# Delta net preparation: sums of squares from transposed tiles, by ScalarE squares, GpSimd halving additions and a VectorE reduction

## Chip, cores, metric

One core of a Trainium2 chip. The metric is the device time of one execution in microseconds (us), the median of several runs.

## What is computed

One inference step of a hybrid decoder layer for 1024 prompt tokens and 8 decode tokens. The change lies in the gated delta net, in the preparation of its 4 heads of width 128 (the sequence in 8 chunks of 128 tokens here):

```
def l2norm(a):
    return af * lax.rsqrt(jnp.sum(af * af, axis=-1, keepdims=True) + NORM_EPS)
q = l2norm(qkv[..., :GDN_WIDTH].reshape(bsz, T, GDN_HEADS, GDN_HEAD_DIM))
k = l2norm(qkv[..., GDN_WIDTH:2 * GDN_WIDTH].reshape(bsz, T, GDN_HEADS, GDN_HEAD_DIM))
...
L = jnp.where(strict, jnp.einsum('nbhid,nbhjd->nbhij', k_beta, k) * decay, 0.0)
sol = lax.linalg.triangular_solve(L + jnp.eye(C, dtype=f32), rhs, left_side=True, lower=True,
                                  unit_diagonal=True)
qk = jnp.where(tri, jnp.einsum('nbhid,nbhjd->nbhij', q, k) * decay, 0.0)
```

The kernel does not normalise `q` and `k` themselves. It needs, for each token and head, the sum of squares of the query and of the key (`ssq`, `ssk`, one column of 128 tokens per chunk), and puts the factors in later.

## The kernel before

The layer runs in stages: input projections and convolutions together with the S5 part (to about 239 us), the preparation of the delta net (239 to 277), the inversion of the triangular blocks with the `z` projection beside it (to about 328), the merge of the inverted blocks, the chain over the chunks, output projection, norm and the two feed-forward products (to 1273).

`mixers` (line 1210) sets the order around the change. It weaves `gdn_prep` for the 4 heads with the rest of the last convolution tile, `conv_tile(11)` (line 1217): each `yield` of `gdn_prep` gives a cost, and for 0.3 of it the convolution may put in matmuls, in groups of three (lines 155 to 157). Then come `gdn_invert` (line 396), the `z` tiles woven with `gdn_values` (line 1221), and `gdn_merge` (line 436). PE runs in the order written out (a manual schedule, line 1308); the other engines' queues are ordered by the framework's scheduler. SP's queue, which issues the DMAs, is in order too.

`gdn_prep` works on each head in two halves of 4 chunks, so on 8 halves in turn. A half does this:

1. PE transposes 4 chunks of the queries into a PSUM bank `pc`; ScalarE squares each of the four 128x128 blocks and accumulates along the row into `ssq` (line 337). The squares themselves go into a scratch tile `pt` that nobody reads; it is one buffer for both engines that use it.
2. PE transposes the broadcast decay column into a second bank `pc`; ScalarE takes four Relu (line 347), GpSimd subtracts the mask (line 349), ScalarE takes the exponential (line 350): the tile `d2`.
3. PE computes keys by keys and keys by queries, 2 chunks to a bank (lines 359, 360). VectorE multiplies the keys-by-keys block with the identity and accumulates along the row, which gives the diagonal, `ssk` (line 363, four instructions a half).
4. VectorE works out the small factors of 4 columns (lines 368 to 372), GpSimd the power `n4` (line 373), and VectorE scales and masks the products into the tile `uq` (line 377, four instructions a half).

There are 2 banks for `pc`, 4 for the products (`psum(2, 4, 2)`, line 1306), 4 buffers of `d2`. A bank of products is free when `uq` has been written from it.

In `gdn_invert` SP stores the diagonal blocks of `uq` to memory (`du`, 4 DMAs a half) and GpSimd clears them in place once stored (line 408, 4 memsets a half); then `pu` is loaded back, `py` is loaded with unit matrices, and VectorE inverts in 62 instructions (lines 419, 421). `pu` and `py` take buffers of the kind `cv`, of which there are 2 and which the convolution's input also uses: `py` can be loaded when the last convolution's VectorE instructions (line 304) are done.

## Time and profile before

| | |
|---|---|
| median of 3 runs (lowest, highest) | 1276.69 us (1273.3, 1277.96) |
| the profiled execution's own time | 1274.82 us |
| its span | 1273.0 us |
| TensorE clock granted, mean share | 0.98 |
| PE busy | 1211.3 us, 95% |
| VectorE (DVE) busy | 840.5 us, 66% |
| ScalarE (ACT) busy | 639.1 us, 50% |
| GpSimd (POOL) busy | 512.2 us, 40% |

The profile gives, for one execution, the busy time of each engine, the chain of work that ended last, and each instruction with its line, start, duration and the wait before it. A busy share over the whole span is an average of stages with different limits; the rows below cut it by stage. `PEld` is TensorE's weight load, `POOL` is GpSimd, `SPq` is SP's queue of DMA issues. A duration can overlap the next instruction's a little.

### The profile page before, as it was taken

To read this page: it belongs to the slowest core of one execution; us is meant where nothing else is said; L and a number is where in the kernel's file an instruction comes from. 1 tells how busy PE (TensorE), PEld (TensorE's weight loads), DVE (VectorE), ACT (ScalarE), POOL (GpSimd) and SP (SyncE) were. 2 spreads that over 40 slices of the span, in tenths; PEclk is the share of its full clock that TensorE was granted. 3 is DMA by queue.
4 is the path that set the end of the run, shared out by engine and by line. 5 is a ranking of instruction groups with operands and counts; after the bars stand their busy time and mean duration, and the time that the engine had idled before them with its cause. 6 is when DMAs were issued, how large, how long until landed. Compare 5 with 4: busy or idle time off the path is not lost.

```text
span 1273.0 us, 25185 instructions
## 1 busy us (share of the span) xinstructions
PE 1211.3 (95%) x9268; PEld 1179.5 (93%) x9268; DVE 840.5 (66%) x1744; ACT 639.1 (50%) x1458; POOL 512.2 (40%) x540
## 2 busy tenths in 40 slices
PE   8999999889899899989999999999989999999996
PEld 7999999889899799988899999999989999999996
DVE  6477787789626885887734434443886868676667
ACT  5377676763556751367655555555554334242201
POOL 6242333362113760544533232333456632374214
PEclk9999999999969999999999999999999999999998
DMA  7323222122431253013434444544864435252202
GB/s 209 103 77 90 69 72 81 39 71 81 147 102 41 68 190 109 1 55 115 153 129 158 142 174 143 175 142 148 258 201 125 151 108 172 76 161 82 65 34 101
DMA packets 110075, 147.02 MB, mean 115 GB/s; under 512 B 30312, under 2 KB 65528, under 8 KB 109952
## 3 DMA queue, kind: packets, MB, share of 16 engines
q1 hardware_dynamic: 109952, 145.41, 36.6%
q8 instruction: 73, 1.20, 0.4%
q14 instruction: 50, 0.41, 0.1%
HBM read 100.31 MB, written 43.88 MB: 113 GB/s over the span
## 4 chain that ended last, share of the span: by engine, by line
PE 69%; DVE 15%; DMA 7%; issue 4%; ACT 4%; POOL 1%; SPq 1%; POOLq 0%; DVEq 0%; ACTq 0%
PE sb L1441 35%; PE mm L155 7%; PE mm L157 7%; PE mm L156 7%; DMA hst<-ht 2%; DMA hst<-hd 2%; PE mm L1715 1%; PE mm L1717 1%; PE mm L1716 1%; DVE xB L1153 1%; DVE acc L1139 1%; DVE wlo L113 1%; DVE cx L304 1%; DVE uq L377 1%; DVE t L113 1%
## 5 line engine op out<-in xcount | busy, mean ns | idle before, releaser
L113 POOL TENSOR_TENSOR wlo<-wraw,whi 128x512 fp32r<-128x512 f32 (+1 forms) x103 | 129.4, 1258 | 198.4 <-ACT whi L112 151.1
L112 ACT ACTIVATE whi<-wraw 128x512 fp32r<-128x512 f32 (+2 forms) x194 | 112.9, 583 | 168.1 <-PE sb L1441 107.7
L1441 PE MATMUL sb<-t,whi 128*128 128x258 f32 x1008 | 164.4, 286 | 6.2 <-ACT whi L112 3.7
L1441 PEld LDWEIGHTS sb<-t,whi 128*128 128x128 f32 x1008 | 139.9, 191 | 8.1 <-ACT whi L112 4.5
L1441 PE MATMUL sb<-xT,whi 128*128 128x258 f32 x832 | 133.7, 283 | 0.0
L155 PE MATMUL mm<-xhi,whi 128*128 128x344 f32 x384 | 126.4, 329 | 2.7 <-DVE zt L322 2.1
L157 PE MATMUL mm<-xhi,wlo 128*128 128x344 f32 x384 | 123.8, 322 | 0.0
L156 PE MATMUL mm<-xlo,whi 128*128 128x344 f32 x384 | 123.8, 322 | 0.0
L1441 PEld LDWEIGHTS sb<-xT,whi 128*128 128x128 f32 x832 | 114.3, 189 | 0.0
L1669 DVE TENSOR_TENSOR acc<-acc,sb 128x516 f32<-128x516 f32 x112 | 75.9, 685 | 53.6 <-PE sb L1441 53.5
L1441 PE MATMUL sb<-t,wlo 128*128 128x258 f32 x504 | 101.0, 285 | 2.7 <-DVE wlo L113 2.7
L1441 PE MATMUL sb<-xB,whi 128*128 128x258 f32 x624 | 100.3, 283 | 0.0
L113 DVE TENSOR_TENSOR wlo<-wraw,whi 128x512 fp32r<-128x512 f32 (+2 forms) x91 | 67.2, 741 | 43.1 <-ACT whi L112 42.9
L1441 PEld LDWEIGHTS sb<-xB,whi 128*128 128x128 f32 x624 | 85.9, 190 | 0.0
L1441 PE MATMUL sb<-xT,wlo 128*128 128x258 f32 x416 | 83.7, 283 | 0.0
L1441 PEld LDWEIGHTS sb<-t,wlo 128*128 128x128 f32 x504 | 78.3, 191 | 3.4 <-DVE wlo L113 3.4
L112 ACT ACTIVATE t<-hst 128x516 fp32r<-128x516 f32 x84 | 52.6, 633 | 52.1 <-DMA hst<-ht 24.8
L155 PEld LDWEIGHTS mm<-xhi,whi 128*128 128x128 f32 x384 | 72.2, 188 | 4.7 <-DVE zt L322 2.9
L156 PEld LDWEIGHTS mm<-xlo,whi 128*128 128x128 f32 x384 | 72.3, 188 | 0.4 <-issue 0.4
L157 PEld LDWEIGHTS mm<-xhi,wlo 128*128 128x128 f32 x384 | 72.2, 188 | 0.4 <-issue 0.4
L113 POOL TENSOR_TENSOR t<-hst,t 128x516 fp32r<-128x516 f32 x36 | 52.7, 1472 | 34.7 <-ACT t L112 22.8
L1484 DVE TENSOR_TENSOR hst<-sb,hst 128x516 f32<-128x516 f32 x40 | 27.6, 691 | 59.1 <-PE sb L1441 59.1
(512 smaller groups left out, 3535.8 us busy)
## 6 DMA issues: line engine op xcount, KB each, us to landing
hd<-hst SPq DMA_DIRECT2D x52, 258.0 KB
wpair<-in_wff SPq DMA_DIRECT2D x26, 512.0 KB
ht<-hsum SPq DMA_DIRECT2D x48, 258.0 KB
hst<-ht SPq DMA_DIRECT2D x48, 258.0 KB
w2raw<-in_wff SPq DMA_DIRECT2D x64, 192.0 KB
wraw<-in_win SPq DMA_DIRECT2D x40, 256.0 KB
hst<-hd SPq DMA_DIRECT2D x36, 258.0 KB
wraw<-in_wff SPq DMA_DIRECT2D x24, 256.0 KB
```

The costliest lines, as they stand in the source:

```text
L112: nc.scalar.activation(hi, src, AF.Copy)
L113: (lo_eng or nc.vector).tensor_tensor(lo, src, hi.bitcast(F32), op=OP.subtract)
L155: nc.tensor.matmul(ps, hi[:, k % 4, :], mh, start=(k == 0), stop=False)
L156: nc.tensor.matmul(ps, hi[:, k % 4, :], ml, start=False, stop=False)
L157: nc.tensor.matmul(ps, lo[:, k % 4, :], mh, start=False, stop=(k == last))
L304: nc.vector.scalar_tensor_tensor(out, raw[:, j:j + NP], cw[:, t, j:j + 1], out, op0=OP.mult, op1=OP.add)
L377: V.scalar_tensor_tensor(u[:, cc], ps[cc // 2][:, cc % 2], self.s2[:, hc:hc + 1], dt[:, cc, None, :].to_broadcast([128, 2, 128]), op0=OP.m ...
L1139: V.scalar_tensor_tensor(x, x, self.lnp[:, 0, i:i + 1], rb, op0=OP.mult, op1=OP.mult)
L1153: nc.vector.scalar_tensor_tensor(lo, x, b, hi.bitcast(F32), op0=OP.add, op1=OP.subtract)
L1441: self.nc.tensor.matmul(ps[:, 512 * c:512 * c + CH], a[:, k, :], forms[c][k][b], start=(start and k == 0 and a is hi and b == 0), stop=(st ...
L1484: V.tensor_tensor(h3, self.banks(ps), h3, op=OP.add)
L1669: V.tensor_tensor(a, a, self.banks(ps), op=OP.add)
```

## The change

A new helper, `squares`, takes the sum of squares of a transposed tile: one large ScalarE square from PSUM into a tile `t`, on GpSimd two additions that fold each group of 128 columns to 64 and to 32 in place, and a VectorE reduction over the last 32. The queries go through it as one tile of 512 columns (a buffer of `d2`). The keys are now transposed as well, four chunks into a third turn of `pc`, and go through it as two tiles of 256 columns (`x1`). The four products with the identity on VectorE and the accumulating squares on ScalarE are gone, and with them this use of `pt`. The new block has a `yield` of its own, of 0.43.

```
+    def squares(self, p, c0, t, out):
+        nc = self.nc
+        n = t.shape[-1]
+        nc.scalar.activation(t, p[:, c0:c0 + n], AF.Square)
+        t3 = t.rearrange("p (c d) -> p c d", d=128)
+        for m in (64, 32):
+            nc.gpsimd.tensor_tensor(t3[:, :, 0:m], t3[:, :, 0:m], t3[:, :, m:2 * m], op=OP.add)
+        nc.vector.tensor_reduce(out, t3[:, :, 0:32], axis=mybir.AxisListType.X, op=OP.add)
+
     def gdn_prep(self, h, q, k, uq):
...
-            for i in range(4):
-                hc = 8 * h + 4 * half + i
-                nc.scalar.activation(self.tmp("pt", 256, bufs=1)[:, :128], p[:, 128 * i:128 * i + 128], AF.Square,
-                                     accum_out=self.ssq[:, hc:hc + 1])
+            self.squares(p, 0, self.tmp("d2", 512, bufs=4), self.ssq[:, 8 * h + 4 * half:8 * h + 4 * half + 4])
...
             yield 0.86
+            p = self.pch()
+            for i in range(4):
+                c = 4 * half + i
+                nc.tensor.transpose(p[:, 128 * i:128 * i + 128], k[:, 128 * c:128 * c + 128], self.ident)
+            for j in range(2):
+                hc = 8 * h + 4 * half + 2 * j
+                self.squares(p, 256 * j, self.tmp("x1", 256, bufs=4), self.ssk[:, hc:hc + 2])
+            yield 0.43
             ps = []
...
-                for i in range(2):
-                    hc = 8 * h + 4 * half + 2 * j + i
-                    V.scalar_tensor_tensor(self.tmp("pt", 256, bufs=1)[:, :128], p[:, i, 0, :], 1.0, self.ident,
-                                           op0=OP.mult, op1=OP.mult, accum_out=self.ssk[:, hc:hc + 1])
                 yield 0.86
```

How the instructions stand now, at two places. First GpSimd's queue at the start of the preparation (`ncp` is the last row of the stage ahead; `d` with `maskneg` is the mask, `n` the power, `uq` the memsets). Before:

```order
L298 TENSOR_SCALAR ncp<-craw 128x3
L349 TENSOR_TENSOR d_3037<-d_3037,maskneg 128x512
L373 TENSOR_TENSOR n_648<-n_648,phalf 128x4
L349 TENSOR_TENSOR d_3097<-d_3097,maskneg 128x512
L408 MEMSET uq 32x4x32 x2
L373 TENSOR_TENSOR n_648<-n_648,phalf 128x4
```

The same place with the change (line 333 is the halving addition, 355 the mask, 383 the power):

```order
L298 TENSOR_SCALAR ncp<-craw 128x3
L333 TENSOR_TENSOR d_3028<-d_3028 128x4x64
L333 TENSOR_TENSOR d_3028<-d_3028 128x4x32
L355 TENSOR_TENSOR d_3034<-d_3034,maskneg 128x512
L333 TENSOR_TENSOR x_3053<-x_3053 128x2x64
L333 TENSOR_TENSOR x_3058<-x_3058 128x2x64
L333 TENSOR_TENSOR x_3053<-x_3053 128x2x32
L333 TENSOR_TENSOR x_3058<-x_3058 128x2x32
L383 TENSOR_TENSOR n_648<-n_648,phalf 128x4
L333 TENSOR_TENSOR d_3095<-d_3095 128x4x64
L333 TENSOR_TENSOR d_3095<-d_3095 128x4x32
L355 TENSOR_TENSOR d_3101<-d_3101,maskneg 128x512
```

Six additions stand in each half, two of them ahead of the mask and the others ahead of the power, which needs VectorE's reduction of them.

Second VectorE's queue at the last half (`cq`, `n`, `s`, `edec` are the small factors), where the last convolution's instructions (line 304) stand. Before (363 is the product with the identity, 368 to 372 the small factors, 377 `uq`):

```order
L363 SCALAR_TENSOR_TENSOR pt,ssk<-ps,ident 128x128
L372 TENSOR_SCALAR cq<-ssq 128x4
L363 SCALAR_TENSOR_TENSOR pt,ssk<-ps,ident 128x128 x3
L368 TENSOR_SCALAR n_648<-ssk 128x4
L369 RECIPROCAL s_645<-n_648 128x4
L370 TENSOR_TENSOR s_645<-s_645,beta 128x4
L371 TENSOR_TENSOR edec<-s_645,edl 128x4
L377 SCALAR_TENSOR_TENSOR uq<-ps,s_645,d_3456 128x256 x4
L304 SCALAR_TENSOR_TENSOR cx<-craw,wconv,cx 128x1024 x3
```

With the change (334 is the reduction, 378 to 382 the small factors, 387 `uq`):

```order
L387 SCALAR_TENSOR_TENSOR uq<-ps,s_645,d_3423 128x256 x4
L304 SCALAR_TENSOR_TENSOR cx<-craw,wconv,cx 128x1024
L334 TENSOR_REDUCE ssq<-d_3483 128x4
L304 SCALAR_TENSOR_TENSOR cx<-craw,wconv,cx 128x1024
L382 TENSOR_SCALAR cq<-ssq 128x4
L334 TENSOR_REDUCE ssk<-x_3508 128x2
L304 SCALAR_TENSOR_TENSOR cx<-craw,wconv,cx 128x1024
L334 TENSOR_REDUCE ssk<-x_3513 128x2
L378 TENSOR_SCALAR n_648<-ssk 128x4
```

Before, the three convolution instructions stood behind the eighth half's `uq`; now they stand between its reductions.

## Rows read from the trace of the kernel before

**Rows 1.** The page: busy time of PE and of GpSimd with their share of the span and number of instructions, and the chain that ended last by engine.

```profile
PE 1211.3 (95%) x9268; PEld 1179.5 (93%) x9268; DVE 840.5 (66%) x1744; ACT 639.1 (50%) x1458; POOL 512.2 (40%) x540
PE 69%; DVE 15%; DMA 7%; issue 4%; ACT 4%; POOL 1%; SPq 1%; POOLq 0%; DVEq 0%; ACTq 0%
```

**Rows 2.** Busy time by stretch: the preparation, the inversion, the end of the `z` tiles. The columns: the stretch and its length, then busy us (and instructions) of PE, PEld, DVE, ACT, POOL, the granted TensorE clock as a share of full speed, the DMA engines' busy share, GB/s.

```profile
239.00:277.00 38.00, 33.00 (x251) 30.66 (x250) 32.00 (x136) 29.62 (x114) 24.60 (x44) 1.00 0.12 20
...
286.00:318.00 32.00, 29.91 (x191) 28.98 (x190) 29.96 (x70) 10.56 (x28) 8.19 (x6) 1.00 0.27 81
318.00:333.00 15.00, 13.77 (x98) 13.23 (x97) 5.92 (x25) 7.21 (x18) 6.11 (x6) 1.00 0.49 131
```

**Rows 3.** The chain of waits through 225 to 345 us, in order of time: start, length, what.

```profile
253.46 1.65 DVE uq L377 x4
...
275.55 1.42 DVE uq L377 x4
...
281.93 4.09 DMA py<-in_eye
```

**Rows 4.** The timeline of single engines in the preparation and just behind it: start, duration, engine, line, in brackets the idle time before and its releaser.

```profile
239.46 0.27 ACT L337 ACTIVATE pt<-pc 128x128 f32<-128x128 f32 x1
...
252.07 0.16 DVE L370 TENSOR_TENSOR s<-s,beta 128x4 f32<-128x4 f32 x1
252.26 1.27 DVE L371 TENSOR_TENSOR edec<-s,edl 128x4 f32<-128x4 f32 x1
...
252.24 1.28 POOL L349 TENSOR_TENSOR d<-d,maskneg 128x512 f32<-128x512 f32 x1 [1.10 <-ACT d L347]
...
274.75 0.19 DVE L368 TENSOR_SCALAR n<-ssk 128x4 f32<-128x4 f32 x1
275.47 1.65 DVE L377 SCALAR_TENSOR_TENSOR uq<-ps,s,d 128x256 f32<-128x256 f32 x4
277.04 4.83 DVE L304 SCALAR_TENSOR_TENSOR cx<-craw,wconv,cx 128x1024 f32<-128x1024 f32 x3
...
277.18 2.29 POOL L113 TENSOR_TENSOR wlo<-wraw,whi 128x512 fp32r<-128x512 f32 x1
```

**Rows 5.** GpSimd's groups of instructions by line and shape: number, busy us, mean ns of one, idle before; the last row is the view of one tile, with the shortest, median and longest of its instructions in ns (the two of 128x8 are the shortest).

```profile
L113 POOL TENSOR_TENSOR msl<-ysr,msh 128x256 fp32r<-128x256 f32 x8 | 6.9, 902 | 1.5 <-ACT msh L112 1.4
L349 POOL TENSOR_TENSOR d<-d,maskneg 128x512 f32<-128x512 f32 x8 | 10.2, 1277 | 12.5 <-ACT d L347 10.9 <-DMA du<-uq 1.4
L373 POOL TENSOR_TENSOR n<-n,phalf 128x4 f32<-128x4 f32 x8 | 8.1, 1013 | 2.5 <-DVE s L369 2.0
L408 POOL MEMSET uq<- 32x128 f32 x32 | 6.4, 199 | 4.8 <-DMA du<-uq 1.8 <-PE pc L343 1.7
L568 POOL TENSOR_TENSOR sso<-sso,mhalf 128x1 f32<-128x1 f32 x32 | 17.7, 556 | 1.9
L1810 POOL TENSOR_TENSOR yt<-yt,gb 128x256 f32<-128x256 f32 x2 | 1.4, 723 | 0.2
...
L113 POOL TENSOR_TENSOR msl<-ysr,msh x10: 232/870/1094, 416.5 to 425.4; 128x256 fp32r<-128x256 f32 x8, 128x8 fp32r<-128x8 f32 x2
```

**Rows 6.** GpSimd's timeline where one operation reads the result of the one before it.

```profile
435.72 0.27 POOL L567 TENSOR_SCALAR sso<-sso,cq 128x1 f32<-128x1 f32 x1
436.07 0.55 POOL L568 TENSOR_TENSOR sso<-sso,mhalf 128x1 f32<-128x1 f32 x1
```

**Rows 7.** Groups by line and shape of ScalarE and VectorE, columns as in rows 5.

```profile
L1421 ACT ACTIVATE hst<-mm 128x258 f32<-128x258 f32 x24 | 9.0, 373 | 4.5 <-PE mm L157 4.2 <-DMA wraw<-in_wff 0.3
L337 ACT ACTIVATE pt<-pc 128x128 f32<-128x128 f32 x32 | 9.0, 280 | 2.7 <-DVE pt L363 2.0
L337 ACT ACTIVATION_READ_ACCUMULATOR pt<-pc 128x1 f32 x32 | 6.4, 201 | 0.0
L956 ACT ACTIVATE T<-pc 128x512 f32<-128x512 f32 x8 | 4.7, 593 | 2.6 <-PE pc L955 2.6
...
L363 DVE SCALAR_TENSOR_TENSOR pt<-ps,ident 128x128 f32<-128x128 f32 x32 | 9.2, 289 | 5.5 <-ACT pt L337 4.3
L929 DVE TENSOR_TENSOR pc<-bw,bw 128x64 f32<-128x64 f32 x8 | 1.7, 218 | 0.0
```

**Rows 8.** PE's timeline at the starts of two neighbouring halves without a wait: the query transposes.

```profile
249.63 0.60 PE L334 MATMUL pc<-ident,cx 128*128 128x128 f32 x4
...
253.50 0.60 PE L334 MATMUL pc<-ident,cx 128*128 128x128 f32 x4
```

**Rows 9.** The hand-over from the last half to the inversion: SP's queue of DMA issues (start, length of the issue) and VectorE's first instruction of the inversion.

```profile
277.15 2.11 SPq L407 DMA_DIRECT2D du<-uq  x4
...
281.21 0.32 SPq L410 DMA_DIRECT2D pu<-du  x1
281.93 0.33 SPq L412 DMA_DIRECT2D py<-in_eye  x1
...
286.12 0.21 DVE L419 TENSOR_TENSOR pt<-pu,py 128x31 f32<-128x31 f32 x1 [2.27 <-DMA py<-in_eye]
```

**Rows 10.** Busy time by stretch in the merge, columns as in rows 2.

```profile
346.00:350.00 4.00, 2.32 (x25) 1.77 (x24) 3.33 (x6) 3.32 (x7) 0.00 (x0) 0.70 0.00 0
350.00:354.00 4.00, 4.00 (x40) 4.00 (x39) 1.23 (x1) 2.04 (x6) 0.00 (x0) 0.50 0.02 4
...
370.00:374.00 4.00, 4.00 (x26) 4.00 (x26) 1.07 (x5) 1.45 (x5) 0.00 (x0) 0.81 0.01 2
```

## Prediction

> **What bounds the kernel now.** I read the page's totals and the chain that ended last first: PE is busy 95% of the span and GpSimd 40%, and of the chain 69% is PE and 15% VectorE [rows 1]. Averages hide the stage that the change touches, so I cut the span into stages. In the preparation, 239 to 277 us, VectorE is busy 32.0 of 38 us, PE 33.0, ScalarE 29.6 and GpSimd 24.6 [rows 2]: no engine has much room, and GpSimd has the most. The chain through this stage shows who sets the pace: the groups of four scaled copies (`uq`, line 377) on VectorE. The third half-head's begins at 253.46 and the eighth's at 275.47, so five halves take 22.0 us, 4.40 us each [rows 3, 4]. Behind the eighth stand the last convolution's three VectorE instructions, the load of `py` and the inversion, whose first instruction starts at 286.12 [rows 3, 4, 9]. In the stretches 286 to 318 and 318 to 333 PE lives on the `z` tiles [rows 2]; the merge behind them needs the inversion's result. What delays the eighth `uq` group therefore delays the inversion, the merge and all that follows. There is no slack behind the merge to give it back: from there the chain runs on PE to the end.
>
> **Step 1: ScalarE and VectorE get lighter.** Four squares with their accumulator reads (0.28 and 0.20 us, partly overlapped, about 0.41 a pair by their starts, so 1.6 us a half) go for one 512-wide square (as line 956, 0.59) and two 256-wide ones (as line 1421, 0.37): 1.3 us [rows 7]. ScalarE gains 0.3 us a half. VectorE loses four products with the identity (0.29 each and 0.05 to the next, 1.36 us) and gets three reductions over 128, 64 and 64 elements. No row has a reduction; line 929 handles 64 elements in 0.22 us [rows 7], and I take 0.7 us for the three. VectorE gains 0.65 us of 4.40. Bounds: a gain of 1.0 if a reduction cost only 0.12, a loss of nothing if it cost 0.45.
>
> **Step 2: PE gets four transposes of keys a half.** Four transposes hold PE for at most 0.60 us; a half without waits took from 249.63 to 253.50, 3.87 us [rows 8]. 3.87 + 0.5 = 4.4 us: PE alone could still keep the old pace. The transposes need a third turn of the two `pc` banks in a half, freed by ScalarE in its order; ScalarE has the room. The three matmuls of the last convolution that are drawn into the preparation only change places. I cost step 2 at nothing as long as GpSimd is slower than 4.4 us.
>
> **Step 3: GpSimd gets six additions a half, and this is the term that decides.** Their sizes are 256, 128, twice 128 and twice 64 elements. No row of before has the small sizes, but 512 elements take 1.28 us (line 349), 256 take 0.72 (line 1810) and the smallest of 8 elements 0.23 [rows 5]. That is 0.18 us and 2.15 ns an element: 0.73, 0.46 and 0.32 us. A half adds 0.73 + 3 x 0.46 + 2 x 0.32 = 2.75 us. To that come what GpSimd did already: the mask 1.28, the power 1.01 and four memsets of 0.20 = 3.1 us [rows 5]. Sum 5.85 us a half against a pace of 4.40: GpSimd, the engine with the most room, becomes the slowest.
> The floor is six times 0.23 = 1.4 us, the ceiling takes 0.90 for 256 elements (the slow form of line 113) and 0.556 for the others (line 568), 3.7 us [rows 5]. I take the line through three sizes, since the new instructions are the same operation between its points.
> The Trainium skill, GPSIMD Engine Reference, section 3.1, prices a two-input operation at about 2.6 cycles an element at 1.2 GHz, with dispatch left unpriced. By that alone the six additions would be an estimated 1.7 us a half, and the kernel about 8 us faster than by my sum; the row of 8 elements at 0.23 us shows that the fixed share is there, so I stay with the rows.
>
> **Step 4: the sum.** In its new order GpSimd does, from the first square to the last halving addition: eight masks 10.2, 48 additions 22.0, seven powers 7.1, 24 of the 32 memsets 4.8, one weight split 1.3: 45.4 us. The first square begins at 239.46 [rows 4] and now ends some 0.6 later, at 240.1. Three kinds of waits come on top. The first power stands right behind the first half's additions and waits for VectorE's reduction and reciprocal, about 0.9. An addition that reads the one before it starts after that one's end, as the power at 436.07 starts 0.08 us after the operation before it ends [rows 6]; some dozen such places, 1.0. And the convolution's three VectorE instructions now stand between the last half's reductions; a GpSimd instruction beside one of them took 2.29 us for 1.28 [rows 4]; I take one such hit, 1.0. So the last addition ends at 240.1 + 45.4 + 2.9 = 288.4. VectorE then reduces (0.2), does its four small operations (0.72, from 274.75 to 275.47) and `uq` (1.65) [rows 4]. The small ones with two SBUF inputs can wait out a GpSimd operation: line 371 took 1.27 us beside the mask at 252.24, where line 370 took 0.16 just before [rows 4]; I add 0.6 for one partial hit. Eighth `uq` done: 291.6 against 277.1, **14.5 us later**.
> The hand-over to the inversion hardly changes. Before, the stores of `uq` began at 277.15, `pu` was loaded at 281.21 and `py` at 281.93, and VectorE started at 286.12, 9.0 us after `uq` [rows 9]. `py` had to wait for the convolution; now `pu` and `py` go out one after the other, 0.4 us better. Inversion: 14 us later. PE's other stream suffers alike: SP sends its queue in order, and the second `z` tile's weights stand behind those stores and loads, so the `z` tiles end about as much later. Merge and all behind it: +14 us.
> The profiled execution took 1274.82 us (span 1273.0): 1288.8. The median of the three runs, 1276.69, lies 1.9 above it; so I forecast **1290 us**.
>
> **The rivals.**
> A. *The additions are hidden.* If six additions cost no more than 1.3 us a half, GpSimd stays within 4.4 us and VectorE's relief shows. The deciding point is 0.22 us an addition, just under the smallest 8-element row. PE at 4.4 us then sets the pace, so at most 8 x 0.1 us are gained, with 0.4 at the hand-over and at most the 2.0 us that ScalarE waited for VectorE through the shared `pt` buffer [rows 7], 3 us in all: 1272 to 1277 us, not slower. For it: GpSimd is busy only 24.6 of 38 us. Against it: the size-dependent rows. Chance 0.10.
> B. *The additions cost the floor or a little more.* 1.4 to 2.0 us a half: 4.5 to 5.1 us a half, 34 to 39 us of work, the waits as above: +3 to +8 us, 1279 to 1285. Chance 0.13.
> C. *PE's clock falls as well.* PE would be kept waiting a quarter of each half, and again between the first and second `z` tile. Before, the granted clock fell to 0.70 in 346 to 350, in which PE was busy 2.32 of 4 us, was 0.50 (1.2 GHz) from 350, and 0.81 in 370 to 374 [rows 10]: some 22 us at half speed. The same once more while the `z` tiles run alone would cost up to 11 us on top: 1294 to 1302. Against it: in the preparation PE's waits are spread thin, and what the `z` tiles lose counts only beyond the inversion's own delay. Chance 0.14.
> That the change doesn't do what it says cannot be: the scheduler's order lists the 48 additions there, ahead of powers and masks.
>
> **How the numbers follow.** My forecast, GpSimd as the bound with +8 to +20 us, gets 0.61; A 0.10, B 0.13, C 0.14, and 0.02 stays for a gain that no row supports. The range takes the additions from just above their floor (5 us over the sum's base: 1281) to the ceiling (3.7 us a half, 8 x 0.95 = 7.6 us more, and a short fall of the clock: 1302). A measurement of this kernel can tell about 0.5%, 6.4 us. Slower by more than that: the forecast, C and half of B, 0.82. Within it: A and the other half of B, 0.16. Faster by more: 0.02.
>
> **What would show it.** In the changed profile GpSimd should be busy almost without a gap from 240 to 288 us, with additions near 0.73, 0.46 and 0.32 us; `uq` groups about 5.9 us apart; VectorE idle behind GpSimd's additions; the inversion's start near 300; PE with gaps in the preparation at the banks that `uq` frees. I am wrong if the additions come in at 0.25 us (then A or B), if `uq` keeps its 4.4 us, or if the merge starts no later although the inversion does.

## The result, and the profile after

The changed kernel took **1292.76 us** (median of 4 runs, 1292.2 to 1293.26). The kernel before, run beside it, took 1274.99 us (4 runs, 1272.93 to 1277.96). The ratio is 1.014, with a 95% interval of 1.0124 to 1.0155: slower. The profiled execution took 1292.2 us with a span of 1290.5, against 1274.82 and 1273.0 before. So the change costs 17.8 us. A second set of runs later gave 1291.26 us and 1.0118 (1.009 to 1.0145).

The page of the changed kernel, totals and the chain by engine, which answer to [rows 1]:

```profile
PE 1220.0 (95%) x9300; PEld 1190.1 (92%) x9300; DVE 838.8 (65%) x1704; ACT 637.6 (49%) x1418; POOL 529.2 (41%) x588
...
PE 73%; DVE 10%; DMA 5%; issue 3%; POOL 3%; ACT 3%; SPq 1%; POOLq 0%; DVEq 0%; ACTq 0%
```

The totals hide the change almost wholly: GpSimd's share went from 40% to 41%. The chain gives GpSimd 3% where it had 1%. The stages show it. These are busy times of the changed kernel by stretch (columns as in [rows 2]): the preparation, the hand-over to the inversion, the inversion with the `z` tiles.

```profile
239.00:294.00 55.00, 46.30 (x332) 44.04 (x330) 36.71 (x99) 31.07 (x79) 47.88 (x98) 0.95 0.11 21
294.00:303.00 9.00, 3.78 (x13) 3.78 (x14) 4.12 (x15) 0.22 (x1) 0.00 (x0) 0.62 0.39 136
303.00:335.00 32.00, 31.97 (x208) 31.62 (x207) 24.75 (x58) 11.33 (x30) 8.36 (x6) 1.00 0.34 111
```

In the preparation GpSimd is now the busiest engine, 47.9 of 55 us, where it was the least busy, 24.6 of 38 [rows 2]. Below are GpSimd's groups of the changed kernel between 236 and 290 us (number, busy us, mean ns of one, idle before). `d` in line 333 holds the squares of queries, `x` those of keys; a shape such as 128x64 is two pieces of 32 columns for `x` and would be four of 16 for `d`.

```profile
L355 POOL TENSOR_TENSOR d<-d,maskneg 128x512 f32<-128x512 f32 x8 | 10.2, 1273 | 0.1
L383 POOL TENSOR_TENSOR n<-n,phalf 128x4 f32<-128x4 f32 x8 | 8.2, 1023 | 0.9 <-DVE s L379 0.8
L333 POOL TENSOR_TENSOR x<-x 128x128 f32<-128x128 f32 x16 | 7.0, 460 | 0.1
L333 POOL TENSOR_TENSOR d<-d 128x256 f32<-128x256 f32 x8 | 5.9, 733 | 8.7 <-ACT d L330 8.5
L333 POOL TENSOR_TENSOR x<-x 128x64 f32<-128x64 f32 x16 | 5.7, 366 | 0.4
...
L333 POOL TENSOR_TENSOR d<-d 128x128 f32<-128x128 f32 x8 | 3.6, 456 | 0.5
```

The additions take 733, 456 to 460 and 366 ns, 22.2 us together, and GpSimd is almost never idle before one of these (of the 8.7 us, 7.9 are its wait for the first squares). From 244 to 286 us it is busy 39.4 of 42 us, more than any other engine. The mask, which waited 12.5 us before [rows 5], waits 0.1 us. VectorE now waits instead. Its reductions in the changed kernel, from 236 to 292 us:

```profile
L334 DVE TENSOR_REDUCE ssk<-x 128x2 f32<-128x64 f32 x16 | 3.5, 218 | 9.8 <-POOL x L333 8.9 <-ACT d L330 0.7
...
L334 DVE TENSOR_REDUCE ssq<-d 128x4 f32<-128x128 f32 x8 | 2.2, 280 | 7.0 <-POOL d L333 7.0
```

VectorE's timeline of the changed kernel (start, length) shows the first `uq` group, the longest of the small operations of line 381 (0.16 us at its shortest), and the end of the stage with the start of the inversion:

```profile
242.83 1.66 DVE L387 SCALAR_TENSOR_TENSOR uq<-ps,s,d 128x256 f32<-128x256 f32 x4
...
267.69 1.72 DVE L381 TENSOR_TENSOR edec<-s,edl 128x4 f32<-128x4 f32 x1
...
285.70 2.26 DVE L304 SCALAR_TENSOR_TENSOR cx<-craw,wconv,cx 128x1024 f32<-128x1024 f32 x1
287.88 0.20 DVE L334 TENSOR_REDUCE ssk<-x 128x2 f32<-128x64 f32 x1
...
288.94 1.66 DVE L387 SCALAR_TENSOR_TENSOR uq<-ps,s,d 128x256 f32<-128x256 f32 x4
298.54 0.20 DVE L429 TENSOR_TENSOR pt<-pu,py 128x31 f32<-128x31 f32 x1 [7.94 <-DMA py<-in_eye]
298.66 0.50 DVE L322 SCALAR_TENSOR_TENSOR zt<-zt,mm 128x344 f32<-128x344 f32 x1
```

The first `uq` group starts at 242.83 and the eighth at 288.94: seven steps of 6.59 us on average (4.1 to 8.3), where the same seven steps took 4.48 us before (244.09 to 275.47; the last five of them are the 4.40 of [rows 3, 4]). VectorE's timeline of the kernel before, its first `uq` group and its first `z` evacuation:

```profile
244.09 1.66 DVE L377 SCALAR_TENSOR_TENSOR uq<-ps,s,d 128x256 f32<-128x256 f32 x4
...
283.34 0.51 DVE L322 SCALAR_TENSOR_TENSOR zt<-zt,mm 128x344 f32<-128x344 f32 x1 [1.47 <-ACT zt L315]
```

The eighth `uq` ends at 290.60, before at 277.12: **13.5 us later**. SP's queue of the changed kernel between `uq` and the inversion, which answers to [rows 9]:

```profile
290.62 1.75 SPq L417 DMA_DIRECT2D du<-uq  x4
293.60 0.34 SPq L420 DMA_DIRECT2D pu<-du  x1
294.04 0.38 SPq L422 DMA_DIRECT2D py<-in_eye  x1
```

From the end of `uq` to the inversion's first instruction it is 7.9 us, before 9.0. Something that the prediction did not have stands in the last two rows of VectorE's timeline of the changed kernel. The first evacuation of a `z` tile (line 322) now stands behind the inversion's first instruction in VectorE's queue, where before it stood ahead of it (283.34, the inversion's first at 286.12 [rows 9]). TensorE's timeline of the changed kernel shows what waited, and ahead of it the first transposes of the values, which waited for a bank that the seventh `uq` group frees:

```profile
281.54 0.66 PE L399 MATMUL ps<-ident,cx 128*128 128x128 f32 x4 [2.33 <-DVE uq L387]
...
299.22 0.66 PE L155 MATMUL mm<-xhi,whi 128*128 128x344 f32 x1 [7.48 <-DVE zt L322]
```

And by stretch, again of the changed kernel:

```profile
292.00:296.00 4.00, 0.00 (x0) 0.00 (x0) 0.00 (x0) 0.92 (x4) 0.79 (x4) 1.00 0.40 107
296.00:300.00 4.00, 0.78 (x3) 0.78 (x4) 1.36 (x6) 0.00 (x0) 0.00 (x0) 0.53 0.41 166
300.00:304.00 4.00, 4.00 (x18) 4.00 (x18) 3.66 (x13) 0.63 (x1) 0.46 (x1) 0.62 0.28 92
304.00:308.00 4.00, 4.00 (x28) 4.00 (x27) 3.86 (x6) 0.98 (x2) 2.49 (x2) 1.00 0.20 66
```

TensorE stands for 7.5 us; its granted clock reads 0.53 over 296 to 300 us, near half (1.2 GHz), still 0.62 over the next 4 us, in which TensorE is busy without a gap, and full again (2.4 GHz) from 304. The merge's first matmul starts at 342.7, before at 328.2: 14.5 us later, with the last `uq` 13.5 us later.

TensorE does the transposes of the values and the `z` tiles, then the merge. In the kernel before, the first of these transposes stands here:

```profile
274.73 0.60 PE L389 MATMUL ps<-ident,cx 128*128 128x128 f32 x4
```

The last `z` matmul ends 1.1 us ahead of the merge in both kernels, while the inversion ends 10.6 us ahead of it before and 14.5 us in the changed kernel. So it is TensorE's own row of work that the merge follows. It starts 6.8 us later (281.54 against 274.73) and takes 7.7 us longer (61.2 us against 53.5): 5.4 us more of waits for `z` evacuations and 2.7 us more outside all waits, which I read as the lower clock, less another wait of 0.5 us. From the merge to the end of the span the changed kernel took 947.8 us and the kernel before 944.8; the repeats below come back to these 3 us.

### The profile page after: what moved, and what is told of

It reads as the page before. It is cut to its first block, busy times and chain, and to the rows that moved or that the text cites. A ratio compares the mean times of both kernels' runs of the same rounds, so it can differ in the third digit from the quotient of the medians.

```text
span 1290.5 us, 25219 instructions
## 1 busy us (share of the span) xinstructions
PE 1220.0 (95%) x9300; PEld 1190.1 (92%) x9300; DVE 838.8 (65%) x1704; ACT 637.6 (49%) x1418; POOL 529.2 (41%) x588
## 4 chain that ended last, share of the span: by engine, by line
PE 73%; DVE 10%; DMA 5%; issue 3%; POOL 3%; ACT 3%; SPq 1%; POOLq 0%; DVEq 0%; ACTq 0%
PE sb L1451 35%; PE mm L155 8%; PE mm L157 7%; PE mm L156 7%; DMA hst<-ht 2%; PE mm L1725 1%; PE mm L1727 1%; PE mm L1726 1%; DVE xB L1163 1%; DMA hst<-hd 1%; DVE acc L1149 1%; DVE t L113 1%; DVE wlo L113 1%; DVE cx L304 1%; PE mm L142 1%
## 5 line engine op out<-in xcount | busy, mean ns | idle before, releaser
L112 ACT ACTIVATE t<-hst 128x516 fp32r<-128x516 f32 x84 | 52.6, 633 | 52.2 <-DMA hst<-ht 27.9
```

What stands on the lines that cost most here:

```text
L112: nc.scalar.activation(hi, src, AF.Copy)
```

## The experiments

My theory: GpSimd's work per half sets the pace of the preparation, the last `uq` sets the merge, and the merge the end. The first rival: the transposes and large squares cost it. The second: the new place of the `z` evacuation does.

**No halving.** GpSimd's additions are left out and VectorE reduces all 128 squares of a row; transposes and large squares stay.

```
-        for m in (64, 32):
-            nc.gpsimd.tensor_tensor(...)
-        nc.vector.tensor_reduce(out, t3[:, :, 0:32], ...)
+        nc.vector.tensor_reduce(out, t3, ...)
```

> The changed kernel without the two halving additions on GpSimd: VectorE reduces the squares over all 128 columns itself. Large squares and transposed keys stay. Theory GpSimd (its additions set the pace): groups of uq come 4.3 to 4.6 us apart instead of 6.0, VectorE being the slowest again with about 1.3 us of reductions a half, and the time is 1271 to 1279 us. Rival theory transposes (the key transposes, the third turn of the two PSUM banks and the large squares make the delay): uq stays at 5.5 us or more, the time at 1286 or more.

Measured: 1275.25 us, ratio 1.0013 (0.9992 to 1.0033). The whole loss is gone without GpSimd's additions, so they are its cause. With them goes the long wait at the hand-over too: the first `z` evacuation stands ahead of the inversion in VectorE's queue again, at 280.74. So this run leaves out the second rival as well and does not tell how much of the loss went by it. VectorE's timeline of this kernel, the start of the first `uq` group and the last group:

```profile
241.44 0.88 DVE L385 SCALAR_TENSOR_TENSOR uq<-ps,s,d 128x256 f32<-128x256 f32 x2 [0.66 <-ACT d L354]
...
273.54 1.66 DVE L385 SCALAR_TENSOR_TENSOR uq<-ps,s,d 128x256 f32<-128x256 f32 x4
```

Its eight groups stand 4.6 us apart (241.44 to 273.54), within 0.1 us of the kernel before. Transposes, large squares and VectorE's longer reductions, in place of the products with the identity, cost nothing on balance and gain nothing either. Busy times of this kernel by stretch suggest why: TensorE has 31.25 of 32 us, so I read it that the four added transposes took the room that the lighter engines gave.

```profile
243.00:275.00 32.00, 31.25 (x255) 30.19 (x254) 29.14 (x86) 20.86 (x59) 21.12 (x41) 1.00 0.10 16
```

**One halving.** The changed kernel with the first addition alone; VectorE reduces 64.

```
-        for m in (64, 32):
+        for m in (64,):
...
-        nc.vector.tensor_reduce(out, t3[:, :, 0:32], ...)
+        nc.vector.tensor_reduce(out, t3[:, :, 0:64], ...)
```

> The changed kernel with one halving addition instead of two (128 columns to 64), VectorE reduces 64. GpSimd's additions are 0.73 + 2 x 0.46 = 1.65 us a half, with its other work 4.75. Theory GpSimd: uq groups 4.8 to 5.1 us apart, time 1277 to 1284 us, between the kernel before and the changed one. Rival theory transposes: 6.0 us apart, above 1288.

Measured: 1281.52 us, ratio 1.0059 (1.0035 to 1.0082). The time is in the expected range. The groups stand 5.58 us apart (243.42 to 282.45), about half a microsecond over the 4.8 to 5.1 expected. I had counted GpSimd's work alone, 4.75 us a half; from 243 to 282 us GpSimd was busy 32.8 of 39 us, so it was no longer full, and what it and VectorE waited for in turn (its longest waits were for ScalarE's squares, 2.5 us) had no place in my sum.

**Three halvings.** The other way.

```
-        for m in (64, 32):
+        for m in (64, 32, 16):
...
-        nc.vector.tensor_reduce(out, t3[:, :, 0:32], ...)
+        nc.vector.tensor_reduce(out, t3[:, :, 0:16], ...)
```

> The changed kernel with a third halving (32 to 16 elements) on GpSimd, so that VectorE reduces 16 per row block. If GpSimd's work per half sets the pace of the preparation: three additions more per half, by the trend 733, 460, 366 ns of 256, 128, 64 elements about 0.30 + 2 x 0.27 = 0.85 us, so the eight uq groups stand some 7.3 to 7.6 us apart in place of 6.59, the last uq ends 6 to 8 us later than in the changed kernel, and the time is 1297 to 1302. If it is the first z evacuation's place in VectorE's queue that costs the time and the pace is hidden: 1291 to 1295, as the changed kernel.

Measured: 1295.63 us (1293.22 to 1299.59), ratio 1.0175 (1.0143 to 1.0206). The median lies between the two expectations, so the time alone does not decide; the trace does. The groups stand 7.28 us apart (243.84 to 294.83), the last `uq` ends 5.9 us later than in the changed kernel and the merge starts 6.4 us later: pace and last `uq` are just short of the first expectation. From there to the end of the span it took 942.2 us, 5.6 less than the changed kernel's 947.8, in stages that neither edit touches (see the repeats below). GpSimd's additions in this kernel, 230 to 300 us:

```profile
L333 POOL TENSOR_TENSOR x<-x 128x128 f32<-128x128 f32 x16 | 7.1, 457 | 0.1
L333 POOL TENSOR_TENSOR d<-d 128x256 f32<-128x256 f32 x8 | 5.8, 728 | 8.2 <-ACT d L330 7.8
L333 POOL TENSOR_TENSOR x<-x 128x64 f32<-128x64 f32 x16 | 5.6, 358 | 0.6
...
L333 POOL TENSOR_TENSOR x<-x 128x32 f32<-128x32 f32 x16 | 3.8, 253 | 0.0
L333 POOL TENSOR_TENSOR d<-d 128x128 f32<-128x128 f32 x8 | 3.6, 455 | 0.1
L333 POOL TENSOR_TENSOR d<-d 128x64 f32<-128x64 f32 x8 | 3.6, 449 | 0.1
```

Put side by side, with GpSimd's additions per half from the means of each kernel:

| halvings | additions, us a half | `uq` groups apart | last `uq` ends | merge starts | from `uq` to merge |
|---|---|---|---|---|---|
| none (before) | 0 | 4.48 | 277.1 | 328.2 | 51.1 |
| none | 0 | 4.59 | 275.2 | 326.5 | 51.3 |
| one | 1.64 | 5.58 | 284.1 | 335.4 | 51.3 |
| two (the change) | 2.84 | 6.59 | 290.6 | 342.7 | 52.1 |
| three | 3.77 | 7.28 | 296.5 | 349.1 | 52.6 |

The means of 64 columns hold a few disturbed additions: the median is 0.32 us for the two pieces of `x` as for the four of `d`, and the mean of 449 ns comes from a single addition of 1.36 us among eight.

From row to row, each microsecond of additions a half adds 0.6 to 0.85 us to the half's pace. These are single profiles: the four other profiles with the changed kernel's preparation gave 6.71 to 6.96 us, and the second one of the kernel before 4.63, so the order of the rows stands, and the slopes are rough. The stretch from `uq` to merge hardly changes; two profiles of the kernel before differ in it by 1.2 us (51.08 and 52.25).

**The `z` evacuations elsewhere.** Three kernels try to take the new wait away. In the first, only the first `z` tile's evacuations go to ScalarE and GpSimd:

```
-            if ZE:
+            if h == 0:
```

> The changed kernel, but the first z tile (head 0) leaves PSUM by ScalarE and GpSimd, so that none of its three evacuations stands on VectorE behind the inversion's first instruction. Theory queue (the first z evacuation waits on VectorE behind an instruction that waits for the load of py; PE is idle 7.5 us for it and the z tiles, not the inversion, then set the merge): that idle time is gone, the z tiles end 3 to 7 us sooner, the merge starts when the inversion's result is there, and the time is 1286 to 1290 us. Rival theory inversion (the later inversion alone delays the merge): 1291 to 1294, no change, though PE's gap is gone.

Measured: 1293.28 us, ratio 1.016 (1.0108 to 1.0211), in the range expected if the inversion sets the merge. But the run doesn't tell the two apart, since the wait only moved to the second `z` tile. TensorE's timeline:

```profile
316.29 0.66 PE L155 MATMUL mm<-xhi,whi 128*128 128x344 f32 x1 [8.14 <-DVE zt L322]
```

So all twelve evacuations were moved, in the changed kernel and, as a control, in the kernel before:

```
-ZE = 0
+ZE = 1
```

> The changed kernel with all twelve z evacuations taken from VectorE's queue: ScalarE copies the PSUM tile and GpSimd does the product and the addition, so that none can stand behind the inversion's instructions. The GpSimd pace of the preparation is untouched: the last uq ends near 290.6 us as before this edit. If the z tiles in VectorE's queue set the start of the merge, the 7.5 us gap on TensorE before the first or second z tile goes, the merge then starts some 10.5 to 11 us after the inversion's end as in the kernel before, near 339 to 340 in place of 342.7, and the time is 1287 to 1290. If what the inversion hands on sets it, the merge stays at 342 to 343 and the time is 1291 to 1294. If GpSimd's z work (24 instructions of 344 elements) slows VectorE's inversion, the inversion is longer than its 29.6 us and the time is 1294 or more.

> The kernel before with the same move of all twelve z evacuations to ScalarE and GpSimd: the control of the run above. If VectorE's queue delays the z tiles only in the changed kernel: no difference, 1272 to 1277. If they are delayed in the kernel before as well: 1268 to 1272. If GpSimd's z work slows the inversion: 1277 to 1282, and the run above then has the same 3 to 7 us in it.

Measured: 1300.31 us, ratio 1.0202 (1.0178 to 1.0227), and for the control 1282.63 us, ratio 1.0061 (1.0038 to 1.0085). Each is 7.6 us slower than without the move, the outcome that I had put down to a slower inversion (the control 0.6 us above its range). The inversion is indeed slower: in the first it takes 36.7 us from 301.8 to 338.4 where it took 29.7, its 62 instructions 34.5 us where they took 25.1, with GpSimd busy 19.4 us beside it where it was busy 5.9. In the control it takes 39.2 us for 31.5. What I had not expected is the way by which this reaches TensorE. SP's timeline of the kernel with the change:

```profile
318.02 0.33 SPq L323 DMA_DIRECT2D zd<-zt  x1
338.44 0.32 SPq L432 DMA_DIRECT2D dy<-py  x1
338.86 0.38 SPq L323 DMA_DIRECT2D zd<-zt  x1
```

and ScalarE's, where the evacuation of the next tile waits for its buffer:

```profile
341.88 0.46 ACT L318 ACTIVATE zt<-mm 128x344 f32<-128x344 f32 x1 [14.03 <-DMA zd<-zt]
```

The inversion's store `dy` stands ahead of the `z` stores in SP's queue, so no `z` buffer came free from 318 to 338 us. TensorE then waited 11.3 us for ScalarE (9.4 us in the control), and the merge began 11.7 us after the inversion's end (11.8 in the control). The pair tells of this new wait and not of the old one.

The last attempt writes the first `z` block out ahead of the inversion in the changed kernel:

```
+        self.ahead(zf, 3.0)
         dy = self.gdn_invert(uq)
```

> The changed kernel with the first z block written out ahead of the inversion, so that its evacuation stands ahead of the inversion's first instruction in VectorE's queue (one group of value transposes comes after that block on TensorE; nothing else of the order there changes). The GpSimd pace is untouched: the last uq still ends near 290.6 us. If the evacuation that stood behind the inversion's wait costs the time: the 7.5 us gap on TensorE at 299 us goes, the first evacuation ends near 292 in place of 299, the z tiles and the merge come 3 to 6 us earlier (merge from 337 to 340 in place of 342.7), and the time is 1286 to 1290. If what comes after the inversion sets the merge: merge within 1 us of 342.7 and 1291 to 1295. If the gap comes back at the second block, as in the run that moved only one head's evacuations: also 1291 to 1295, and that gap shows it.

Measured: 1293.55 us, ratio 1.0147 (1.012 to 1.0175). VectorE's timeline shows the edit at work, the first evacuation at 291.43 and the second among the inversion's instructions:

```profile
291.43 0.50 DVE L322 SCALAR_TENSOR_TENSOR zt<-zt,mm 128x344 f32<-128x344 f32 x1
299.55 0.20 DVE L429 TENSOR_TENSOR pt<-pu,py 128x31 f32<-128x31 f32 x1 [7.62 <-DMA py<-in_eye]
...
302.71 0.51 DVE L322 SCALAR_TENSOR_TENSOR zt<-zt,mm 128x344 f32<-128x344 f32 x1
```

and TensorE's timeline shows the wait again, one block later:

```profile
303.27 0.65 PE L155 MATMUL mm<-xhi,whi 128*128 128x344 f32 x1 [6.81 <-DVE zt L322]
```

The merge started at 343.4, 51.9 us after the last `uq`, as without the edit. So the wait that I hadn't foreseen can be moved but did not pay when moved. What it costs is not shown, since no run removes it. The table, in which `uq` to merge grows by 1 us, does not price it: that stretch hardly differs (51.1 to 52.6) between kernels in which TensorE waits 2.1 us and 9.9 us for `z` evacuations. An upper bound can be estimated. The inversion's result alone would have let the merge begin no earlier than about 336.8 (its end at 328.2, and 8.6 us, the shortest way from there to the merge in any profile here, that of the sums on TensorE below), so up to 5.9 of the 14.5 us may hang on the wait. I read its cause so: between `uq` and the inversion VectorE stands 8 us, and TensorE can run ahead only as far as its banks go. In the kernel before, the last convolution's work lay in that hand-over (its VectorE instructions begin at 277.04 [rows 4]). In the changed one it was done by 288, because the scheduler had put it between the last half's reductions.

**Sums on TensorE.** In the kernel before, ScalarE squares queries and keys as they lie (two 512-wide instructions a half), TensorE sums by eight matmuls a half with a column of ones, VectorE reads the sums from PSUM; no transposed queries, no products with the identity.

```
+            sq = [self.tmp("d2", 512, bufs=4) for _ in range(2)]
+            for z, x in zip(sq, (q, k)):
+                nc.scalar.activation(z, x[:, 512 * half:512 * half + 512], AF.Square)
...
+            ss = self.pch()
+            for j in range(2):
+                for i in range(4):
+                    nc.tensor.matmul(ss[:, 4 * j + i:4 * j + i + 1], sq[j][:, 128 * i:128 * i + 128],
+                                     self.ones[:, 0:1], start=True, stop=True)
...
+            V.tensor_scalar(n4, ss[:, 4:8], 1e-6, None, op0=OP.add)
```

> Another way to the same sums, from the kernel before: ScalarE squares queries and keys as they lie in SBUF (two instructions of 128x512 a half), PE multiplies the squares with a column of ones (eight small matmuls a half into one PSUM bank), VectorE's small operations read that bank. No query or key transposes, no accumulating squares, no products with the identity, no additions on GpSimd. Theory VectorE and GpSimd as the bounds: both are relieved (VectorE by 1.4 us a half), uq groups come 3.9 to 4.2 us apart, PE being the slowest, and the time is 1268 to 1274 us. Rival: PE's eight small matmuls cost as much as the transposes or more, uq at 4.4 us or above, 1274 to 1278.

Measured: 1281.68 us, ratio 1.0064 (1.0045 to 1.0084). Both ranges of time missed; of the rival, the pace came true (`uq` 5.0 us apart) and cost more than I had put on it. TensorE's timeline and its busy time by stretch in this kernel:

```profile
248.21 0.60 PE L338 MATMUL pc<-ident,gc 128*128 128x128 f32 x4
248.64 1.84 PE L349 MATMUL pc<-ones,d 128*128 128x1 f32 x16
250.35 0.41 PE L155 MATMUL mm<-xhi,whi 128*128 128x344 f32 x1
```

```profile
248.00:282.00 34.00, 34.00 (x293) 33.94 (x292) 18.78 (x63) 19.44 (x49) 20.54 (x40) 1.00 0.10 15
```

The eight matmuls of one column stand as 16 records and hold TensorE from 248.64 to 250.35: 0.107 us a record, as much as each of the four of 128 columns ahead of them (0.43 us for four by the starts). The 1.71 us are more than the 0.43 of four transposes that they replace, and TensorE is busy all 34 of 34 us: a half takes 4.96 us (248.64 to 253.60) where it took 4.48. The kernel took work off VectorE and ScalarE and made TensorE the bound.

**Scratch of its own.** In the kernel before, ScalarE's squares and VectorE's products write to the same scratch buffer that nobody reads. VectorE gets another:

```
-                    V.scalar_tensor_tensor(self.tmp("pt", 256, bufs=1)[:, :128], ...
+                    V.scalar_tensor_tensor(self.tmp("x1", 256, bufs=4)[:, :128], ...
```

> The kernel before with VectorE's products with the identity written to a scratch buffer of their own (four in turn), where before they shared the one buffer with ScalarE's squares and each side waited for the other (the trace of before shows ScalarE waiting 2.0 us and VectorE 4.3 us on it in the preparation). If these waits pace the halves: uq groups 4.1 to 4.3 us apart in place of 4.48, the last uq 1.5 to 3 us earlier, 1271 to 1273. If VectorE's or TensorE's own work paces them: 1273 to 1277, no difference.

Measured: **1271.7 us** (12 runs), ratio 0.9972 (0.9955 to 0.9989): 0.28% faster than the kernel before, a small gain but clear of 1 by its interval. VectorE's timeline of this kernel, first and last group:

```profile
243.07 1.66 DVE L377 SCALAR_TENSOR_TENSOR uq<-ps,s,d 128x256 f32<-128x256 f32 x4 [1.91 <-ACT d L350]
...
269.67 1.66 DVE L377 SCALAR_TENSOR_TENSOR uq<-ps,s,d 128x256 f32<-128x256 f32 x4
```

The groups stand 3.80 us apart, the last `uq` ends 5.8 us earlier and the merge starts 4.7 us earlier. So it was this shared buffer that held the old 4.48 us. How it did so is seen only in part. Of VectorE's 4.3 us of waits for ScalarE, 3.7 are a single one at the start of the stage (241.95); between the first and the eighth group VectorE was busy 28.6 of 31.4 us before and is busy 25.7 of 26.6 now. TensorE's five waits for banks that ScalarE's old squares held are gone, 3.9 us in all, the longest of them in the kernel before:

```profile
268.19 0.65 PE L343 MATMUL pc<-ident,gc 128*128 128x128 f32 x4 [1.65 <-ACT pt L337]
```

Without the shared tile the scheduler also orders the queues of ScalarE and VectorE anew, and no run separates that order from the waits. The two edits together:

> The kernel before with both edits: the scratch of its own for VectorE's products and the first z block ahead of the inversion. TensorE was busy 95% of the time from the last uq to the merge in the run with the scratch alone, where its two longest waits for a z evacuation were 1.8 us together. If these waits are what is left to take: 1269 to 1271. If that stretch is full with TensorE's own work: 1270 to 1273, as with the scratch alone.

Measured: 1274.12 us, ratio 0.9994 (0.9978 to 1.001), above both expectations. The first group of value transposes started at 274.1 in place of 270.5 and the merge at 326.7 in place of 323.5: the `z` block took their place on TensorE, and the longest wait for a `z` evacuation grew to 3.2 us from 1.1. Which of the two costs the time is not shown.

**Repeats.**

> The changed kernel once more, for a second profile. In its first profile the merge began 14.5 us later than in the kernel before and the end came 17.4 us later; 3 us were added behind the merge, in stages that the change does not touch. If they belong to the changed order of the work: again 2 to 4 us between the delay at the merge and the delay at the end (against the kernel before run beside it). If they belong to where the clock happened to fall in that one execution: the merge at 342 to 344 us again, and the stretch from the merge to the end within 2 us of the kernel before.

> The kernel before once more, for a second profile beside the run above. The stretch from the merge's first matmul to the end of the span was 944.8 us in its first profile and 947.8 in that of the changed kernel. If that stretch is the same from execution to execution: 944 to 946 again. If the clock's falls move it: anything from 943 to 948.

Measured: 1291.26 us for the changed kernel and 1275.36 us for the kernel before. From the merge to the end of the span the changed kernel took 946.4 us (345.1 to 1291.5) and the kernel before 948.1 (328.7 to 1276.8). The latter is the 944.8 of the first profile plus 3.3 us: this stretch moves by that much between executions of the same kernel, and 948.1 is at the upper end of what was expected if the clock's falls move it. The merge itself came 16.4 us later (345.1 is 1 us above the expected place), the eighth `uq` 16.6 (it ends at 293.07 and 276.47), the end 14.7. So the 3 us behind the merge in the first pair don't belong to the change. That the clock's falls make them is not shown. From `uq` to merge it is 52.0 us in the changed kernel and 52.2 in the kernel before: the 1 us between them in the first pair is not there in the second. TensorE's row of work starts 11.3 us later here (284.0 against 272.7) and takes 5.0 us longer.

## Why the prediction came out

It forecast 1290 us with a range of 1281 to 1302; 1292.8 were measured. That GpSimd's additions become the bound of the preparation is the mechanism forecast, and it is what the runs show; the way from the last `uq` to the merge is not the one forecast. The agreement is a little better than earned: 1290 was 13.3 us above a median of 1276.69 from three runs, and the measured cost is 17.8 us over 1274.99. By its steps:

- *Step 1* held as to VectorE: the three reductions take 0.28 and twice 0.22 us, 0.72 a half against 0.7 taken. ScalarE's squares were a little dearer than taken: 0.592 and twice 0.398 us by their means, 1.39 a half against 1.3.
- *Step 2*, the transposes at nothing, is borne out by the kernel without halving (1.0013). The condition attached to it fits too: without GpSimd in the way, TensorE at 31.25 of 32 us would have been the next bound.
- *Step 3*: 733, 456 to 460 and 366 ns against 730, 460 and 320 taken. The line was right at the smallest size as well: 14 of the 16 took 0.31 to 0.34 us, as at 269.97. The mean holds two disturbed ones, 0.92 at 283.29 and 0.46 at 285.17, both beside the convolution's VectorE instructions. The line even holds at 32 elements, 253 ns in the kernel with three halvings, where it gives 0.25. The six come to 2.84 us against 2.75. What the Trainium skill's GPSIMD Engine Reference, section 3.1, gives (2.6 cycles an element, dispatch unpriced) would be 1.7 us by my estimate in the prediction; the trace does not agree with that as a whole price and shows the fixed share, 253 ns for 32 elements in the kernel with three halvings. By the element the two agree: 1.7 us over the 768 elements is 2.2 ns, and the line has 2.15. GpSimd's timeline of the changed kernel:

```profile
269.97 0.32 POOL L333 TENSOR_TENSOR x<-x 128x64 f32<-128x64 f32 x1
...
283.29 0.92 POOL L333 TENSOR_TENSOR x<-x 128x64 f32<-128x64 f32 x1
```

- *Step 4, the sum*: from the first square to the end of the last addition 48.3 us were forecast and 48.4 were measured (237.26 to 285.63). The tail behind it I had put too short: 5.0 us in place of 3.2. The third of the convolution's VectorE instructions, 2.26 us beside GpSimd, stands ahead of the last reduction, and I had put such a hit on GpSimd's side. From the first square to the end of `uq` it is 53.3 us, before 37.7: 15.7 longer, against 13.9 by the forecast's own numbers (51.5). On the clock of the trace it is 13.5 later, because this execution reached the first square 2.2 us earlier, where I had put it 0.6 later. That 13.5 lies so near the 14.5 forecast is luck: in the second pair of profiles, in which the kernel before reaches its first square at 237.8 and not at 239.46, `uq` is 16.6 us later.
- *The pace* of 5.9 us a half was too short: 6.59 were measured, and 6.83 in the second profile. GpSimd's work itself came at 6.05 us a half (48.4 over eight), as in the sum; the 5.9 had left out the weight split and the waits that step 4 adds, and the convolution's instructions ahead of the last group.
- *The hand-over* went to 7.9 us from 9.0, a gain of 1.1 where 0.4 was taken (9.1 and 7.6 in the second pair). The inversion started 12.4 us later, not 14.
- *The merge* at +14.5 against +14 was right for a reason that I had wrong. I had the inversion's result set it, and the `z` tiles delayed alike by weights in SP's queue. The inversion's result was stored only 10.6 us later (328.23 against 317.62); it was the `z` tiles, ending 14.4 us later, that the merge followed. They were delayed in two ways: TensorE came to them 6.8 us later, behind a bank that the seventh `uq` frees, and then stood still for 7.5 us, because the first `z` evacuation stood behind the inversion's first instruction in VectorE's queue. That these add up to nearly the delay forecast is luck too.
- *Rival C* came in small: the granted clock did fall, to 0.82 and 0.75 over 280 to 288 us, behind TensorE's wait of 2.33 us, and to 0.53 and 0.62 over 296 to 304. By the 2.7 us that TensorE's work took longer outside its waits it cost some 3 us, an estimate (1.1 in the second pair); a full second fall in the `z` tiles, with its 11 us, did not come. *Rivals A and B* needed cheaper additions than were measured; with one halving, 1.64 us a half, B's time came about (1281.5 in its 1279 to 1285).

That 4.4 us was what the engines' own work needed in the kernel before was also wrong. The same instructions run at 3.80 us once the scratch buffer is not shared, and the buffer was in [rows 7] as two waits, 2.0 us of ScalarE for VectorE and 4.3 of VectorE for ScalarE. I had priced its removal at up to 2.0 us within rival A; the run gave 4.7 us at the merge.

Open: what the 7.5 us wait would be worth if it were removed and not moved (up to 5.9 us by the estimate above), and by which way the shared buffer held the pace.

## What to carry to other kernels

An engine with the most idle time in a stage can still become the bound when small instructions go to it: price them by a line through the sizes that the trace has, fixed share included, and set the engine's sum per turn of the loop against that turn's pace. Look for who waits for whom through a buffer that nobody reads before moving work between engines; here that edit was the only one that gained. An in-order queue behind one waiting instruction (VectorE's behind a load, SP's behind a store) shows up as another engine's wait; here moving the evacuation moved the wait. And ask which row of work the next stage really follows: here it was TensorE's `z` tiles and not the inversion, though both were late.

## What the runs showed of the hardware

- A matmul record of one column took as long on TensorE as one of 128 columns, 0.107 us each by their starts.
- GpSimd's additions follow a line of 0.18 us and 2.15 ns an element down to 32 elements: medians of 0.73, 0.46, 0.32 and 0.25 us for 256, 128, 64 and 32 in the kernel with three halvings. It made no difference whether 64 elements lay in two pieces of 32 or in four of 16. A few are held up far beyond it, the longest 1.36 us for 64.
- VectorE's inversion slowed beside GpSimd's work: its 62 instructions took 34.5 us with GpSimd busy 19.4 us beside them, and 25.1 us with 5.9.
- VectorE's small operations with operands in SBUF can take far longer beside GpSimd's: line 381, 0.16 us at its shortest, averaged 0.55 us over the eight halves of the changed kernel, up to 1.72.
- The stretch behind the merge took 942 to 948 us in the profiled executions of one preparation or another, and differed by 3 us in two executions of the kernel before: differences of that size in a single profile say nothing.
